# Two of four weight sums made by adding transfers, in a hybrid attention and convolution block on one core

## The chip, the core and the metric

One core of a Trainium2 chip runs one launch of the kernel. The metric is device time in microseconds (us) of that core. The kernel before the change took 2040.47 us, the median of 3 runs (2038.33 to 2040.82).

## What is computed

The block works on 256 rows of width 4096, all in float32. Cut to what matters here:

```
xn   = rms_norm(x, norm_in_g)
proj = xn @ w_in                                   # 4096 -> 14336 columns
q, k, v, z_a, a_c, g_c, z_c = split(proj)          # 2048 columns each
y_a = rms_norm(chunked_attention(q, k, v, rel_table)) * silu(z_a)
u   = causal_depthwise_conv31(a_c * sigmoid(g_c))
y_c = rms_norm(silu(layer_norm(u)) @ w_pw + b_pw) * silu(z_c)
h   = x + concat(y_a, y_c) @ w_out                 # 4096 x 4096
h   = h + sigmoid(rms_norm(h) @ w_ple_gate + b) * (p @ w_ple)
out = rms_norm(h) * final_g
```

Nearly all the work is matrix products of 256 rows with large weights that are read once each from HBM.

## The kernel before

**Precision.** Each float32 operand is split into a high part, rounded to the format that TensorE multiplies, and a low part, the rest. A product is three matmuls: high by high, low by high, high by low (`add`, line 365). For weights, `parts_of` (line 199) makes the parts: ScalarE (ACT) casts the tile to `wh` (line 204), VectorE (DVE) subtracts to get `wl` (line 205).

**Pairs.** `mixed_product` (line 327) computes two column blocks of 512 at once, for two halves of 128 rows. It walks over sixteen (for `w_pw` eight) *pairs*: two blocks of 128 rows of the weight matrix, `w0` and `w1`, each a tile of 128 x 2 x 512 with one row block and both column blocks. A pair is a 2 x 2 block product, taken in one of two ways:

- *plain*: eight block products, 24 matmuls (`add_plain`);
- *seven-product*, marked with a star in the orders: seven block products of sums (Winograd's form of Strassen's scheme), 21 matmuls. It needs sums of the activations (the `comb` tiles, made once) and four sums of weight blocks. With w0 = (a, b) and w1 = (c, d), columns side by side, these are a + b, b + d, a + b + d and a + b + d + c.

The sums were made on DVE: lines 426 and 427 write the first two into the tile `ua`, lines 430 and 431 the other two into `ub`. `pair_parts` (line 308) then splits each tile, `uh` by an ACT cast and `ul` by a DVE subtraction (again lines 204 and 205).

**Order.** Lists written out by hand say which pair comes when and which are seven-product; the eight-of-sixteen list used in most of the second half is

```
dense = units("1 0* 3 2* 5 4* 6* 7 8* 9 10* 11 12* 14* 13 15")
```

`first`, `early`, `early_six` and `late` put the marked pairs in the second half of a stage, mostly with a plain pair between two; `final` is like `dense` with seven marked pairs and three left to the end. In all, 122 of the pairs are seven-product ones. The stages are: the convolution's inputs (4 times), queries and keys (4), the pointwise product (2), the gates `z_a` and `z_c` (4, `dense`), `w_out` (4, the first in `late`) and `w_ple_gate` (4, the first in `late`, the last in `final`).

**Buffers.** Pools set how far loads and parts run ahead: `wpool` has 5 buffers for weight tiles `wt` and 3 each for `wh` and `wl`; `upool` has 2 buffers under each of the tags `u` (for `ua` and `ub`), `uh` and `ul`. Weight loads are asked for by SyncE (SP) in lines 403 and 190, in the order of its instruction stream; a load whose buffer is not free yet waits there, and so does all that stands behind it. A scheduler sets the order of each engine's instructions when the program is built, except where the source pins them. GpSimd (POOL) has little to do: a few powers for the norms (`rsqrt`, line 136), four memsets in the bias tiles (line 895).

Of the kernel before, what the change touches and what calls it, by code (L numbers as in the profile page):

```python
# [10 lines left out]
F32 = mybir.dt.float32  # L11
F32R = mybir.dt.float32r
AF = mybir.ActivationFunctionType
ALU = mybir.AluOpType
AX = mybir.AxisListType

P = 128
NB = 512
# [7 lines left out]
def hybrid_block(  # L26
# [23 lines left out]
    nc = tc.nc  # L50
# [17 lines left out]
    def pool(name, bufs, stack=ctx, side=0, **kw):  # L68
        return stack.enter_context(tc.tile_pool(name=name, bufs=bufs, side=sides[side], **kw))
# [13 lines left out]
    upool = pool("upool", 2, first_sums)  # L83
# [15 lines left out]
    def two_columns(w, kb, col, apart):  # L99

        rows = w[kb * P : (kb + 1) * P, :]
        return bass.AP(
            tensor=rows.tensor, offset=rows.offset + col,
            ap=[list(rows.ap[0]), [apart, 2], [1, NB]],
        )
# [76 lines left out]
    def fill(n):  # L182
        for _ in range(min(n, len(later))):
            later.popleft()()
# [123 lines left out]
    def pair_parts(src):  # L308

        tiles = [upool.tile([P, 2, NB], F32R, tag=tag, name=tag) for tag in ("uh", "ul")]  # L310
        return parts_of(src, 2, tiles)[0]

    def units(text):

        return [(int(u.rstrip("*")), u.endswith("*")) for u in text.split()]
# [3 lines left out]
    first = units("0 1 3 5 7 9 11 13 15 2* 8 4* 10 6* 12 14")  # L319
# [7 lines left out]
    def mixed_product(  # L327
        w, col, lhs, comb, order, on_helpers, ahead=None, fills=(0,), on_begin=None, apart=NB,
        left=(), begin=None,
    ):  # L330

        c = [[ps_acc.tile([P, NB], F32, tag="acc", name=f"acc{h}{j}") for j in range(2)] for h in range(NH)]
        helper = {}
        begun, ends = set(), {}  # L340
        n_left = len(left) // 2
        for n, (_, seven) in enumerate(order[: len(order) - n_left]):
            for name in ("P1", "P5", "P6", "P7", "P2", "P3", "P4") if seven else ("P2", "P3", "P4", "X"):
                ends[name] = n
        banks = {"P2": c[0][0], "P3": c[0][1], "P4": c[1][0], "X": c[1][1]}
        made, held = [], []

        def add_left(h, js, out=None, cols=slice(None)):


            for m in range(0, len(held), 2):
                for j in js:
                    dst = c[h][j] if out is None else out[:, cols]
                    for i, (kb, (wh, wl)) in enumerate(held[m : m + 2]):
                        xh, xl = block(kb, h)
                        for kind, (a, b) in enumerate(((xh, wh), (xl, wh), (xh, wl))):
                            pin(
                                nc.tensor.matmul(  # L358
                                    dst, a, b[:, j, cols],
                                    start=out is not None and m + i + kind == 0,  # L360
                                    stop=m + i + 1 == len(held) and kind == 2,
                                )
                            )

        def add(name, x, w2, n, final, kinds=range(3), then=lambda ins: None):

            for kind in kinds:
                a, b = ((x[0], w2[0]), (x[1], w2[0]), (x[0], w2[1]))[kind]
                made.append(
                    nc.tensor.matmul(  # L370
                        banks[name], a, b, start=name not in begun,
                        stop=final and ends[name] == n and kind == 2 and not (left and name in "P2 P3 P4"),
                    )
                )
                begun.add(name)
                then(made[-1])

        def block(kb, h):
            t = lhs[kb // 4]
            return [t[:, kb % 4, q, h * P : (h + 1) * P] for q in range(2)]  # L380

        def add_plain(n, k, wh, wl, **kw):
            pair = order[n][0]
            for j in range(2):
                for h in range(NH):
                    name = (("P2", "P3"), ("P4", "X"))[h][j]
                    add(name, block(2 * pair + k, h), (wh[:, j], wl[:, j]), n, k == 1, **kw)

        done, after = 0, ExitStack()
        if begin:  # L390
            done, behind = begin(add_plain)
            for ins in behind:
                after.enter_context(tc.issue_after(ins.ins))
        last_seven = max((n for n, (_, seven) in enumerate(order) if seven), default=None)
        for n, (pair, seven) in enumerate(order):
            if n < done:
                continue
            if ahead:
                ahead(pair)
            wts = []  # L400
            for k in range(2):
                wt = wpool.tile([P, 2, NB], F32, tag="w", name="wt")
                nc.sync.dma_start(wt, two_columns(w, 2 * pair + k, col, apart))
                wts.append(wt)
            if n >= len(order) - n_left:
                for k in range(2):
                    tiles = left[2 * (n - len(order) + n_left) + k]
                    held.append((2 * pair + k, parts_of(wts[k], 2, tiles and tiles())[0]))
                fill(fills[n % len(fills)])
                continue  # L410
            if not seven:
                for k in range(2):
                    add_plain(n, k, *parts_of(wts[k], 2)[0])
                fill(fills[n % len(fills)])
                continue
            begins = not helper
            if begins:
                for name in ("P1", "P5", "P7", "P6"):
                    helper[name] = ps_tmp.tile([P, NB], F32, tag="tmp", name=f"acc_{name}")
                banks.update(helper)  # L420
            w0, w1 = wts
            ua = upool.tile([P, 2, NB], F32, tag="u", name="ua")
            ub = upool.tile([P, 2, NB], F32, tag="u", name="ub")
            plus = partial(nc.vector.tensor_tensor, op=ALU.add)
            w0h, w0l = parts_of(w0, 1)[0]
            plus(ua[:, 0], w0[:, 0], w0[:, 1])  # L426
            plus(ua[:, 1], w0[:, 1], w1[:, 1])  # L427
            uah, ual = pair_parts(ua)
            w1h, w1l = parts_of(w1, 2)[0]
            plus(ub[:, 0], ua[:, 0], w1[:, 1])  # L430
            plus(ub[:, 1], ub[:, 0], w1[:, 0])  # L431
            ubh, ubl = pair_parts(ub)
            first = len(made)

            def s_of(i):
                t, at = comb[pair] if isinstance(comb, dict) else (comb[pair // 4], pair % 4)
                return [t[:, at + i // 2, q, (i % 2) * P : (i % 2 + 1) * P] for q in range(2)]

            k0, k1 = 2 * pair, 2 * pair + 1
            add("P1", block(k0, 0), (w0h[:, 0], w0l[:, 0]), n, True)  # L440
            add("P5", s_of(1), (uah[:, 0], ual[:, 0]), n, True)
            add("P7", s_of(0), (uah[:, 1], ual[:, 1]), n, True)
            add("P2", block(k1, 0), (w1h[:, 0], w1l[:, 0]), n, True)
            add("P3", s_of(3), (w1h[:, 1], w1l[:, 1]), n, True)
            add("P6", s_of(2), (ubh[:, 0], ubl[:, 0]), n, True)
            add("P4", block(k1, 1), (ubh[:, 1], ubl[:, 1]), n, True)
            if begins and on_begin:
                on_begin()
            if begins:
                tc.add_manual_dep(  # L450
                    made[first].ins, last_transpose[0].ins.name,
                    mybir.DependencyInfo(mybir.DependencyClass.NoSync, mybir.DependencyReason.DATA),
                    reason="transposes before the helpers take their banks",
                )
            if n == last_seven:
                on_helpers(helper)
            fill(fills[n % len(fills)])
        after.close()
        return (c, add_left) if left else c
# [73 lines left out]
    def first_pairs(add):  # L533
# [62 lines left out]
        for n in range(1, n_x + 1):  # L596
# [26 lines left out]
    rows = [(conv_ln_g, KCW), (conv_ln_b, KCW), (b_dw, KCW), (attn_out_g, AW // P),  # L623
            (conv_out_g, KCW), (ple_norm_g, KD)]
# [315 lines left out]
    for c0, order in zip(range(0, CW // NB, 2), point):  # L940
        row = broadcast_row(b_pw, c0 * NB, 2 * NB, tag="stage")
        rows = [row[:, j * NB : (j + 1) * NB] for j in range(2)]
# [191 lines left out]
    rows, fgs = [], []  # L1134

    def on_begin():
        rows.extend(broadcast_row(b_ple_gate, (c0 + j) * NB, NB) for j in range(2))
# [16 lines left out]
    for j in range(2):  # L1154
        wt = wpool.tile([P, 2, NB], F32, tag="w", name="wt")
# [115 lines left out]
```

## Time and profile before

| | us |
|---|---|
| median of 3 runs | 2040.47 |
| the profiled execution | 2039.1 |
| its span in the profile | 2037.3 |
| TensorE (PE) busy | 2019.6 (99%) |
| VectorE (DVE) busy | 1887.9 (93%) |
| ScalarE (ACT) busy | 1200.8 (59%) |
| GpSimd (POOL) busy | 8.1 |
| moved by the DMA engines | 412.29 MB, 202 GB/s over the span |

In a group's row of the profile stand the line, the engine, the operation, the tile written and those read, shapes and count; then busy us and the mean ns of one; then the idle time just before them on that engine and what ended it. A row of a wait table reads: who waited, for whom, us in total, times, longest. A row of the timeline: start, length, engine, line, operation, and in brackets an idle time before it. A row of DMA issues: tile and tensor, the issuing queue, count, KB of each, median us from issue to landing. PEld is TensorE's loading of weights, which runs beside its matmuls; a PE that is busy in the table can still be paced by something else, so the distance from one matmul's start to the next is read from the timeline.

### The profile page before, as it was taken

To read this page: it belongs to the slowest core of one execution; us is meant where nothing else is said; L and a number is where in the kernel's file an instruction comes from. 1 tells how busy PE (TensorE), PEld (TensorE's weight loads), DVE (VectorE), ACT (ScalarE), POOL (GpSimd) and SP (SyncE) were. 2 spreads that over 40 slices of the span, in tenths; PEclk is the share of its full clock that TensorE was granted. 3 is DMA by queue.
4 is the path that set the end of the run, shared out by engine and by line. 5 is a ranking of instruction groups with operands and counts; after the bars stand their busy time and mean duration, and the time that the engine had idled before them with its cause. 6 is when DMAs were issued, how large, how long until landed. Compare 5 with 4: busy or idle time off the path is not lost.

```text
span 2037.3 us, 26041 instructions
## 1 busy us (share of the span) xinstructions
PE 2019.6 (99%) x9106; PEld 1659.5 (81%) x9106; DVE 1887.9 (93%) x2688; ACT 1200.8 (59%) x1559; POOL 8.1 (0%) x19
## 2 busy tenths in 40 slices
PE   9999999999999999999999999999999999999997
PEld 7888888877888888888888888888888888888876
DVE  7999999799989998868899999999999999999998
ACT  7655546554565546676555656676565666655555
POOL 0000000000000000000000000000000000000000
PEclk9999999999999999999999999999999999999999
DMA  8666665666656665655666666676666656666765
GB/s 295 188 200 204 204 187 165 202 191 189 184 185 204 201 188 183 186 184 199 190 216 204 197 216 199 219 238 204 214 201 205 214 185 208 198 221 205 235 208 179
DMA packets 161853, 412.29 MB, mean 202 GB/s; under 512 B 12974, under 2 KB 16190, under 8 KB 161722
## 3 DMA queue, kind: packets, MB, share of 16 engines
q1 hardware_dynamic: 161072, 409.80, 63.3%
q8 instruction: 71, 1.16, 0.2%
q10 hardware_dynamic: 650, 0.84, 0.1%
q14 instruction: 60, 0.49, 0.1%
HBM read 406.39 MB, written 4.19 MB: 202 GB/s over the span
## 4 chain that ended last, share of the span: by engine, by line
PE 86%; DVE 10%; issue 2%; DMA 1%; ACT 1%; POOLq 0%; POOL 0%; ACTq 0%; DVEq 0%
PE acc L370 61%; PE acc_P L370 15%; PE acc L218 7%; DVE wl L205 4%; DVE cv L677 3%; DMA wt<-in_w_in_dram 1%; PE tmp_ps L170 1%; DVE ul L205 1%; PE tmp_ps L867 0%; PE tmp_ps L849 0%; ACT wh L204 0%; PE acc L358 0%; PE tmp_ps L834 0%; DVE z L492 0%; PE tmp_ps L872 0%
## 5 line engine op out<-in xcount | busy, mean ns | idle before, releaser
L370 PE MATMUL acc<-wh,big_t 128*128 128x512 f32 x3788 | 1172.1, 391 | 0.6 <-DVE z L988 0.3
L204 ACT CAST wh<-wt 128x1024 fp32r<-128x1024 f32 (+1 forms) x737 | 715.8, 982 | 543.0 <-PE acc L370 330.6
L205 DVE TENSOR_TENSOR wl<-wt,wh 128x1024 fp32r<-128x1024 f32 (+1 forms) x737 | 825.4, 1132 | 65.0 <-ACT wh L204 60.1
L370 PEld LDWEIGHTS acc<-wh,big_t 128*128 128x128 f32 x3788 | 708.4, 188 | 146.5 <-issue 0.6
L370 PE MATMUL acc<-wl,big_t 128*128 128x512 f32 x1894 | 731.1, 391 | 1.0 <-DVE wl L205 1.0
L370 PEld LDWEIGHTS acc<-wl,big_t 128*128 128x128 f32 x1894 | 355.2, 188 | 76.7 <-DVE wl L205 3.1
L677 DVE SCALAR_TENSOR_TENSOR cv<-uT,dw,cv 128x255 f32<-128x255 f32 (+23 forms) x480 | 204.9, 467 | 1.1
L204 ACT CAST uh<-ub 128x1024 fp32r<-128x1024 f32 x122 | 128.5, 1054 | 126.2 <-DVE ub L431 102.7
L218 PE MATMUL acc<-wh,big_t 128*128 128x512 f32 x560 | 173.1, 390 | 0.0
L204 ACT CAST uh<-ua 128x1024 fp32r<-128x1024 f32 x122 | 128.7, 1055 | 71.7 <-DVE ua L427 63.5
L205 DVE TENSOR_TENSOR ul<-ub,uh 128x1024 fp32r<-128x1024 f32 x122 | 149.0, 1221 | 8.8 <-ACT uh L204 7.8
L370 PE MATMUL acc_P<-uh,big_t 128*128 128x512 f32 x504 | 154.4, 392 | 0.0
L205 DVE TENSOR_TENSOR ul<-ua,uh 128x1024 fp32r<-128x1024 f32 x122 | 148.9, 1220 | 0.4 <-ACT uh L204 0.2
L218 PEld LDWEIGHTS acc<-wh,big_t 128*128 128x128 f32 x560 | 104.8, 188 | 21.4
L370 PEld LDWEIGHTS acc_P<-uh,big_t 128*128 128x128 f32 x504 | 93.3, 188 | 22.2 <-ACT uh L204 3.7
L218 PE MATMUL acc<-wl,big_t 128*128 128x512 f32 x280 | 109.1, 390 | 0.0
L426 DVE TENSOR_TENSOR ua<-wt 128x512 f32<-128x512 f32 x122 | 83.9, 688 | 25.9 <-DMA wt<-in_w_in_dram 19.0
L370 PE MATMUL acc_P<-ul,big_t 128*128 128x512 f32 x252 | 96.8, 392 | 0.0
L427 DVE TENSOR_TENSOR ua<-wt 128x512 f32<-128x512 f32 x122 | 83.7, 686 | 3.9 <-DMA wt<-in_w_in_dram 3.0
L431 DVE TENSOR_TENSOR ub<-ub,wt 128x512 f32<-128x512 f32 x122 | 83.8, 687 | 1.0
L430 DVE TENSOR_TENSOR ub<-ua,wt 128x512 f32<-128x512 f32 x122 | 83.7, 686 | 0.3
L370 PE MATMUL acc<-uh,big_t 128*128 128x512 f32 x244 | 75.4, 390 | 0.0
(241 smaller groups left out, 1523.0 us busy)
## 6 DMA issues: line engine op xcount, KB each, us to landing
wt<-in_w_in_dram SPq DMA_DIRECT2D x447, 512.0 KB, 4.0
wt<-in_w_out_dram SPq DMA_DIRECT2D x128, 512.0 KB, 4.2
wt<-in_w_ple_gate_dram SPq DMA_DIRECT2D x128, 512.0 KB, 4.2
wt<-in_w_pw_dram SPq DMA_DIRECT2D x32, 512.0 KB, 4.5
hc<-in_x_dram SPq DMA_DIRECT2D x8, 512.0 KB, 5.8
wt<-in_w_ple_dram SPq DMA_DIRECT2D x8, 512.0 KB, 4.2
xin<-in_x_dram SPq DMA_DIRECT2D x7, 512.0 KB, 8.2
out_dram<-hc SPq DMA_DIRECT2D x12, 256.0 KB, 2.4
```

Of the source, the lines that this page charges most:

```text
L170: nc.tensor.transpose(pt[:, i * T + h * P : i * T + (h + 1) * P], src[:, h, b * P : (b + 1) * P], ident,)
L204: nc.scalar.copy(wh[:, :kc, :], wt[:, :kc, :]),
L205: nc.vector.tensor_tensor(wl[:, :kc, :], wt[:, :kc, :], wh[:, :kc, :].bitcast(F32), ALU.subtract),
L218: nc.tensor.matmul(acc, a, b[:, k, :], start=kb == 0 and kind == 0, stop=kb == kblocks - 1 and kind == 2,)
L370: nc.tensor.matmul(banks[name], a, b, start=name not in begun, stop=final and ends[name] == n and kind == 2 and not (left and name in "P2 ...
L426: plus(ua[:, 0], w0[:, 0], w0[:, 1])
L427: plus(ua[:, 1], w0[:, 1], w1[:, 1])
L430: plus(ub[:, 0], ua[:, 0], w1[:, 1])
L431: plus(ub[:, 1], ub[:, 0], w1[:, 0])
L677: nc.vector.scalar_tensor_tensor(cv[:, i, PAD - k :], uT[:, i, : T + k - PAD], dw[:, b, k : k + 1], cv[:, i, PAD - k :], ALU.mult, ALU.add,)
```

## The change

Of the four sums of a seven-product pair, the first two (a + b and b + d) are no longer made on DVE. A plain transfer from SP loads (b, b) into `ua`, and a transfer from GpSimd that adds on writing puts (a, d) on top. The new function `sums_ahead(n)` asks for both for every seven-product pair among the next two in the order, right after the weight loads of pair n. As b of `w0` is not needed any more, only a of it is loaded. The other two sums are written over the first two in `ua`, after those have been split; `ub` is gone, and the two buffers of the tag `u` serve the `ua` of two pairs.

```diff
+        sums = {}
+
+        def sums_ahead(n):
+            for m in range(n, min(n + 3, len(order))):
+                if not order[m][1] or m in sums:
+                    continue
+                ua = sums[m] = upool.tile([P, 2, NB], F32, tag="u", name="ua")
+                rows = w[2 * order[m][0] * P : (2 * order[m][0] + 1) * P, :]
+                step = P * rows.ap[0][0]
+
+                def columns(first, step):
+                    return bass.AP(
+                        tensor=rows.tensor, offset=rows.offset + first,
+                        ap=[list(rows.ap[0]), [step, 2], [1, NB]],
+                    )
+
+                nc.sync.dma_start(ua, columns(col + apart, 0))
+                nc.gpsimd.dma_start(ua, columns(col, step + apart), accum_op=ALU.add)
...
-                nc.sync.dma_start(wt, two_columns(w, 2 * pair + k, col, apart))
+                if seven and k == 0:
+                    nc.sync.dma_start(wt[:, 0], w[2 * pair * P : (2 * pair + 1) * P, col : col + NB])
+                else:
+                    nc.sync.dma_start(wt, two_columns(w, 2 * pair + k, col, apart))
                 wts.append(wt)
+            sums_ahead(n)
...
-            ua = upool.tile([P, 2, NB], F32, tag="u", name="ua")
-            ub = upool.tile([P, 2, NB], F32, tag="u", name="ub")
+            ua = sums[n]
             plus = partial(nc.vector.tensor_tensor, op=ALU.add)
             w0h, w0l = parts_of(w0, 1)[0]
-            plus(ua[:, 0], w0[:, 0], w0[:, 1])
-            plus(ua[:, 1], w0[:, 1], w1[:, 1])
             uah, ual = pair_parts(ua)
             w1h, w1l = parts_of(w1, 2)[0]
-            plus(ub[:, 0], ua[:, 0], w1[:, 1])
-            plus(ub[:, 1], ub[:, 0], w1[:, 0])
-            ubh, ubl = pair_parts(ub)
+            plus(ua[:, 0], ua[:, 0], w1[:, 1])
+            plus(ua[:, 1], ua[:, 0], w1[:, 0])
+            ubh, ubl = pair_parts(ua)
```

## The prediction

> **What bounds the kernel now.** I read the page's engine shares first, then TensorE's own waits, then the chain of waits, to learn how much a lighter VectorE could return at all.
>
> ```profile
> span 2037.3 us, 26041 instructions
> PE 2019.6 (99%) x9106; PEld 1659.5 (81%) x9106; DVE 1887.9 (93%) x2688; ACT 1200.8 (59%) x1559; POOL 8.1 (0%) x19
> ```
> ```profile
> PEld acc_P L370 <- ACT uh L204: 4.7, 18, 0.5
> PEld acc_P L370 <- DVE ul L205: 4.0, 14, 0.6
> PEld acc L370 <- DVE wl L205: 3.1, 7, 1.2
> ```
> ```profile
> 1170.85 6.12 PE acc L370 x27
> ```
>
> The reader is to see that PE is the bound and nearly full: it is without work for 2037.3 - 2019.6 = 17.7 us, start and tail included. In the chain, 27 matmuls follow each other in 6.12 us, one per 0.227 us, and that pace hardly breaks. What VectorE (DVE) and ScalarE (ACT) owe PE in weight parts is 4.7 + 4.0 + 3.1 = 11.8 us of late weight loads, part of it hidden behind the matmul before. So a change that only unloads DVE can win a few us; I take 5, between 0 and 11.8. DVE is close behind, though, as three stretches show (columns: stretch; its length, then busy us of PE, PEld, DVE, ACT, POOL; granted clock, DMA share, GB/s):
>
> ```profile
> 0.00:60.00 60.00, 58.67 (x286) 46.88 (x287) 45.94 (x79) 44.65 (x87) 0.89 (x8) 1.00 0.81 272
> 1157.00:1239.00 82.00, 82.00 (x364) 67.91 (x363) 78.70 (x94) 49.59 (x55) 0.00 (x0) 1.00 0.65 206
> 1845.00:1930.00 85.00, 85.00 (x373) 69.26 (x372) 84.31 (x103) 49.13 (x59) 0.00 (x0) 1.00 0.68 214
> ```
>
> The second row is one stage in the order `dense`, eight seven-product and eight plain pairs. There the DMA engines are busy for 0.65 of the time. In the third, a gate stage, DVE works 84.31 of 85 us.
>
> **What the change removes.** Two of four sums in each of 122 pairs, lines 426 and 427:
>
> ```profile
> L426 DVE TENSOR_TENSOR ua<-wt 128x512 f32<-128x512 f32 x122 | 83.9, 688 | 25.9 <-DMA wt<-in_w_in_dram 19.0 <-DMA wt<-in_w_out_dram 4.9 <-DMA wt<-in_w_ple_gate_dram 1.1
> L427 DVE TENSOR_TENSOR ua<-wt 128x512 f32<-128x512 f32 x122 | 83.7, 686 | 3.9 <-DMA wt<-in_w_in_dram 3.0 <-DMA wt<-in_w_out_dram 0.7
> ```
>
> That is 83.9 + 83.7 = 167.6 us of DVE, 11 us per dense stage. It lies beside PE's work, so it returns only the 5 us above. The sums of lines 430 and 431 stay. Written over `ua`, they must now follow ACT's cast and DVE's subtraction that read `ua`; per pair the chain is cast 1.06, subtraction 1.22, two sums of 0.69, cast 1.06, subtraction 1.22 (the timeline rows below), some 5.7 us with their overlaps.
>
> **What it adds in bytes.** A pair loads 0.26 MB less for `w0`, 0.52 MB more for the plain half of `ua` and 0.52 MB more that is added: 0.79 MB, or 6.3 MB per dense stage. At 206/0.65 = 317 GB/s these take 19.8 us, and the DMA share goes from 0.65 to 0.89. Issuing from GpSimd takes no bytes off these engines. [...] No run here shows a GpSimd transfer yet.
>
> The first two `ua` loads stand in SP's queue between the loads of `x`. Four transfers, 2.1 MB, at 272/0.81 = 336 GB/s are 6 us; the first 60 us leave 0.19 x 60 = 11 us free. I cost that at nothing; without that cover it is at most 6 us.
>
> **What it adds in waits.** This is the term that decides. `upool` has two buffers for `ua`, so the `ua` of a pair can be asked for only when the last subtraction (`ul<-ub`) of the seven-product pair before the previous one is done. "Two pairs ahead" is the place in the source; in the order in which SP's instructions stand in the built program, a dense stage asks for the sums of 6* between the two loads of that same pair, and for 8*, 10* and 14* just ahead of their own pair's loads. From the release four things follow in a row: SP's issue, the plain load, GpSimd's issue, the adding transfer. The rows nearest to them:
>
> ```profile
> L403 SPq DMA_DIRECT2D wt<-in_w_in_dram x366: 327/367/371, 45.1 to 1306.2; - x183
> DMA to landing us min/median/max: 3.3/4.1/8.2
> ```
> ```profile
> wt<-in_w_in_dram SPq DMA_DIRECT2D x447, 512.0 KB, 4.0
> xin<-in_x_dram SPq DMA_DIRECT2D x7, 512.0 KB, 8.2
> ```
> ```profile
> L895 POOL MEMSET bias<- 64x256 f32 x4 | 1.2, 306 | 705.2 <-DMA bias<-in_rel_table_dram 477.9 <-ACT wh L204 227.3
> L139 POOL TENSOR_TENSOR r_x<-r_x,mhalf 128x2 f32<-128x2 f32 x1 | 1.0, 1009 | 58.9 <-DVE r_x L138 58.9
> ```
>
> An adding transfer and a GpSimd issue are in no row. Bounds: the adding transfer between the fastest plain one (3.3) and the slowest (8.2), GpSimd's issue between its cheapest instruction (0.3) and its dearest (1.0). Low end: 0.3 + 3.3 + 0.3 + 3.3 = 7.2 us; high end: 0.4 + 8.2 + 1.0 + 8.2 = 17.8. I take 0.4 + 4.0 + 1.0 + 8.2 = 13.6: for the adding one the `xin` row, since those loads ran at a DMA share of 0.81, nearest to the 0.89 worked out above.
>
> How much time the present schedule gives, in the dense stage above: for 6*, 10* and 14*, the release (end of `ul<-ub` of 2*, 6*, 10*), the cast that needs `ua`, the subtraction behind it, and PE's first use of that.
>
> ```profile
> 1176.75 1.22 DVE L205 TENSOR_TENSOR ul<-ub,uh 128x1024 fp32r<-128x1024 f32 x1
> ...
> 1190.81 1.22 DVE L205 TENSOR_TENSOR ul<-ua,uh 128x1024 fp32r<-128x1024 f32 x1
> ...
> 1193.68 1.22 DVE L205 TENSOR_TENSOR ul<-ub,uh 128x1024 fp32r<-128x1024 f32 x1
> ...
> 1205.50 1.22 DVE L205 TENSOR_TENSOR ul<-ua,uh 128x1024 fp32r<-128x1024 f32 x1
> ...
> 1210.58 1.22 DVE L205 TENSOR_TENSOR ul<-ub,uh 128x1024 fp32r<-128x1024 f32 x1
> ...
> 1225.47 1.23 DVE L205 TENSOR_TENSOR ul<-ua,uh 128x1024 fp32r<-128x1024 f32 x1
> ```
> ```profile
> 1189.07 1.06 ACT L204 CAST uh<-ua 128x1024 fp32r<-128x1024 f32 x1 [0.30 <-PE acc_P L370]
> ...
> 1204.03 1.06 ACT L204 CAST uh<-ua 128x1024 fp32r<-128x1024 f32 x1
> ...
> 1224.38 1.06 ACT L204 CAST uh<-ua 128x1024 fp32r<-128x1024 f32 x1 [0.26 <-PE acc_P L370]
> ```
> ```profile
> 1192.90 0.39 PE L370 MATMUL acc_P<-ul,big_t 128*128 128x512 f32 x1
> ...
> 1213.30 0.39 PE L370 MATMUL acc_P<-ul,big_t 128*128 128x512 f32 x1
> ...
> 1228.26 0.39 PE L370 MATMUL acc_P<-ul,big_t 128*128 128x512 f32 x1
> ```
>
> From release to cast: 1189.07 - 1177.97 = 11.1 us for 6*, 1204.03 - 1194.90 = 9.1 for 10*, 1224.38 - 1211.80 = 12.6 for 14*. From subtraction to PE: 0.9, 6.6 and 1.6 us, the slack. At 13.6 us: 6* is 13.6 - 11.1 = 2.5 late, PE waits 2.5 - 0.9 = 1.6. Its release stays 2.4 late (chain 5.7 against 5.8 now), 10* is 2.4 + 4.5 = 6.9 late, inside 6.6 plus the 1.6 that PE has lost already. The release of 10* makes up 2.1 (5.7 against 7.8), 14* is 4.8 + 1.0 = 5.8 late, and PE waits 5.8 - 1.6 - 1.6 = 2.6. Together 4.2 us per dense stage. Nine stages have that order and the last one nearly so: 42 us. The orders `early` and `late` space the marked pairs by a plain pair almost throughout, so I cost them at nothing.
>
> ```profile
> SPq L403 <- DVE wl L205: 1052.4, 478, 9.8
> ```
>
> Queued behind the waits: on ACT, behind the cast of `ua`, stand the `wh` casts of the next pairs, and on DVE their subtractions; that is why a late `ua` makes everything behind it late, and PE waits as soon as the slack is gone. On SP, a `ua` load that waits for its buffer holds back weight loads; the row above shows that SP stands waiting for DVE for half the span already, and the loads are in time. GpSimd's few other instructions (`r_x`, `r_c`, `r_h`, four memsets) stand among the adding transfers; behind `r_h` are sums from the third marked pair of the gate stage on, needed many pairs later: nothing.
>
> **Sum.** The profiled execution took 2039.1 us, span 2037.3 with 1.8 around it; the runs' median, 2040.47, is 1.4 above. 2039.1 + 42 - 5 = 2076 for that execution, and I forecast **2077** for a median.
>
> **Rivals.**
> - *Hidden, faster.* The place is the same chain; it decides at about 12 us from release to landing: PE is first touched by 6* at 11.1 + 0.9 = 12.0, by 14* at 12.2. For it: the low end is 7.2, and with plain times for both transfers (0.4 + 4.1 + 1.0 + 4.1 = 9.6) nothing outruns its slack. Then only the 5 us of late parts go: 2035.
> - *Hidden, no difference.* The same, but PE's own pace hides what DVE gives back: 2037 to 2044.
> - *DMA engines full.* If an added byte costs an engine twice a plain one, eight transfers of 0.52 MB add another 13 us per dense stage: share 0.89 + 0.16 = 1.05. No transfer is quick then, and at the high end, 17.8 us, the same walk gives 6* 5.8, 10* 2.9 and 14* 8.1 us of waiting: 17 us per stage, 170 in all, 2205. Against it: the rows show no engine time of an adding packet. [...]
> - *It does not run ahead.* Already in the forecast: SP's order undoes the two pairs of lead in dense stages.
>
> **How the numbers follow.** Slower with the chain at 12.3 to 16 us: 0.50. At 16 us the walk gives 11 us per stage, 2150. DMA engines full, above that: 0.20. Hidden and faster: 0.17. Hidden and within 0.2%: 0.13; 0.2% is 4 us, about what a measurement of this kernel can tell from no change. Range 2034 to 2180: it takes in about half of the faster case and half of the full-engine case, and leaves some 0.18 out. Faster 0.17, same 0.13, slower 0.70.
>
> **What would show it.** Right: ACT's `uh<-ua` casts waiting for the adding transfer in dense stages, PE waiting for `uh` and `ul` there, GpSimd transfers landing 8 us after issue, DMA share near 0.9. Wrong: landings near 4 us and no new PE wait (hidden), or a DMA share near 1.0 with all weight loads late (full engines). DVE should lose 167 us of busy time in every case.

## The result, and the profile after

The changed kernel takes **2198.67 us** (median of 6 runs, 2190.15 to 2223.04), the kernel before 2040.26 (6 runs, 2038.33 to 2040.82): a ratio of 1.0771, 95% interval 1.0749 to 1.0793, 158 us more. The forecast was 2077, its range 2034 to 2180. The direction was right, the size was not: the result lies 19 us above the range. The longest of the six runs had a lower granted clock (0.978) than the others (0.983 to 0.987) and is left out of the ratio. The profiled execution took 2198.76.

First the page of the changed kernel: engines, then the DMA queues (packets, MB, share of 16 engines' span).

```profile
span 2197.0 us, 26397 instructions
...
PE 2076.5 (95%) x9106; PEld 1665.9 (76%) x9106; DVE 1755.4 (80%) x2444; ACT 1188.9 (54%) x1559; POOL 168.0 (8%) x141
...
q1 hardware_dynamic: 190032, 441.79, 60.3%
q0 software_dynamic: 33184, 63.97, 18.2%
```

PE does the same 9106 matmuls, and now stands without work for 120.5 us where it stood for 17.7. VectorE is 132 us lighter and no longer close to the bound. The new queue q0 holds the adding transfers. It moves 63.97 MB in 0.182 x 16 x 2197.0 = 6398 us of engine time, 0.205 us per 2 KB; q1 needs 0.603 x 16 x 2197.0 = 21197 us for 441.79 MB, 0.098 us per 2 KB. **An added byte cost an engine 2.1 times a plain one.** That is the condition of the rival "DMA engines full", which took the factor as two; this trace shows the factor, and can't show the reason.

Next the issues (KB of each, median us from issue to landing). The weight tiles took 4.0 before.

```profile
wt<-in_w_in_dram SPq DMA_DIRECT2D x382, 512.0 KB, 4.7
...
ua<-in_w_in_dram SPq DMA_DIRECT2D x65, 512.0 KB, 4.9
ua<-in_w_in_dram POOLq DMA_DIRECT2D x65, 512.0 KB, 7.6
```

Then two dense stages in the table by stretches, in the columns of the prediction's. Before, such a stage was 82 us long with a DMA share of 0.65, 53 us of engine time. Now:

```profile
1133.00:1223.00 90.00, 84.75 (x360) 66.36 (x360) 69.38 (x76) 48.09 (x55) 9.74 (x8) 1.00 0.90 257
1223.00:1312.00 89.00, 84.33 (x361) 66.41 (x360) 69.44 (x77) 47.93 (x55) 9.74 (x8) 1.00 0.90 259
```

The share reads 0.90, close to the 0.89 forecast, but of a longer stage: 0.90 x 89 = 80 us of engine time. At the pace of before that would be 80 of 82 us. A share must be turned into time before two stages of different length are compared.

Who waits: ScalarE's cast of the first sums for the transfers, and PE for that cast.

```profile
ACT uh L204 <- DMA ua<-in_w_in_dram: 86.2, 31, 9.5
...
PE acc_P L370 <- ACT uh L204: 41.1, 29, 9.2
```

Matmul by matmul, the loss of 160 us between the two profiled executions stands here: 109 us in the ten stages in the orders `dense` and `final` (10.9 each), 11 in the two in `late` among them, 23 in the first pointwise stage, 14 in the first convolution stage, 3 net in all the rest. The stages in the orders `early` stay within 3 us each, nearly as forecast.

A look at 6* in the second of the two stages shows the chain (timeline; the release is the end of the first row):

```profile
1236.70 1.22 DVE L205 TENSOR_TENSOR ul<-ua,uh 128x1024 fp32r<-128x1024 f32 x1
...
1237.95 0.38 SPq L405 DMA_DIRECT2D ua<-in_w_in_dram  x1
...
1244.01 1.22 POOL L406 DMA_DIRECT2D ua<-in_w_in_dram  x1 [9.34 <-DVE wl L205]
...
1252.13 1.05 ACT L204 CAST uh<-ua 128x1024 fp32r<-128x1024 f32 x1 [2.95 <-DMA ua<-in_w_in_dram]
...
1256.93 1.05 ACT L204 CAST uh<-ua 128x1024 fp32r<-128x1024 f32 x1 [1.86 <-DVE ua L451]
1258.03 0.74 PE L370 MATMUL acc_P<-uh,big_t 128*128 128x512 f32 x2 [0.98 <-ACT uh L204]
```

From release to cast it is 1252.13 - 1237.92 = 14.2 us, forecast 13.6. PE stops briefly for the first sums at 1253.23, and again at 1258.03 for the larger ones, which are made only after the first have been split. That is the chain of the prediction, at about its length. But it does not stand at 6* and 14* alone. In the 86 seven-product pairs that follow the first one of the first `dense` stage, the cast starts within 0.2 us of the landing in 81%: four pairs in five wait for their own transfer. The table of line 406 says the same for the whole run (us waited, times), 77 of 122:

```profile
who waited for it (us, times):
  ACT uh L204: 229.6, 77
```

PE does not pay at each of them. Counted matmul by matmul, of the 109 us in the ten stages 32 stand at 6*, 24 at 14*, 23 at 8*, 21 at 10* and 9 at all other pairs. At 8* and 10* PE is mostly late at the plain parts of the pair's own tiles. Here is such a place at 10* (ScalarE, then PE):

```profile
1185.88 1.05 ACT L204 CAST uh<-ua 128x1024 fp32r<-128x1024 f32 x1 [2.76 <-DVE ua L451]
1186.83 2.94 ACT L204 CAST wh<-wt 128x1024 fp32r<-128x1024 f32 x3
```
```profile
1187.92 0.73 PE L370 MATMUL acc<-wh,big_t 128*128 128x512 f32 x2 [1.03 <-ACT wh L204]
```

The cast of the larger sums comes late, since line 451 makes them late, and the plain parts stand behind it on ScalarE.

### The profile page after: what moved, and what is told of

Same layout as the page of the kernel before. It is cut to its first block, busy times and chain, and to the rows that moved or that the text cites. A ratio compares the mean times of both kernels' runs of the same rounds, so it can differ in the third digit from the quotient of the medians.

```text
span 2197.0 us, 26397 instructions
## 1 busy us (share of the span) xinstructions
PE 2076.5 (95%) x9106; PEld 1665.9 (76%) x9106; DVE 1755.4 (80%) x2444; ACT 1188.9 (54%) x1559; POOL 168.0 (8%) x141
## 2 busy tenths in 40 slices
DMA packets 224000, 508.27 MB, mean 231 GB/s; under 512 B 16878, under 2 KB 20094, under 8 KB 223866
## 3 DMA queue, kind: packets, MB, share of 16 engines
q1 hardware_dynamic: 190032, 441.79, 60.3%
q0 software_dynamic: 33184, 63.97, 18.2%
## 4 chain that ended last, share of the span: by engine, by line
PE 49%; DMA 24%; DVE 14%; issue 7%; ACT 5%; ACTq 0%; SPq 0%; POOLq 0%; DVEq 0%; POOL 0%
PE acc L370 34%; PE acc L218 8%; DMA ua<-in_w_in_dram 8%; DMA ua<-in_w_out_dram 7%; DMA ua<-in_w_ple_gate_dram 6%; DVE wl L205 5%; PE acc_P L370 5%; DVE ul L205 3%; ACT uh L204 3%; DMA wt<-in_w_in_dram 2%; ACT wh L204 2%; DVE ua L451 1%; DVE ua L450 1%; DMA ua<-in_w_pw_dram 1%; DVE cv L697 1%
## 5 line engine op out<-in xcount | busy, mean ns | idle before, releaser
L370 PE MATMUL acc<-wl,big_t 128*128 128x512 f32 x1894 | 743.0, 395 | 15.2 <-DVE wl L205 15.0
L204 ACT CAST uh<-ua 128x1024 fp32r<-128x1024 f32 x244 | 256.3, 1051 | 487.9 <-DVE ua L451 222.4
L205 DVE TENSOR_TENSOR ul<-ua,uh 128x1024 fp32r<-128x1024 f32 x244 | 298.0, 1221 | 254.0 <-ACT uh L204 241.5
L697 DVE SCALAR_TENSOR_TENSOR cv<-uT,dw,cv 128x249 f32<-128x249 f32 (+23 forms) x480 | 201.2, 460 | 1.3
L406 POOL DMA_DIRECT2D ua<-in_w_in_dram x65 | 79.5, 1223 | 943.5 <-DMA ua<-in_w_in_dram 364.8
L218 PE MATMUL acc<-wl,big_t 128*128 128x512 f32 x280 | 109.0, 389 | 0.0
L450 DVE TENSOR_TENSOR ua<-ua,wt 128x512 f32<-128x512 f32 x122 | 83.6, 685 | 11.6 <-DMA wt<-in_w_in_dram 8.8
L451 DVE TENSOR_TENSOR ua<-ua,wt 128x512 f32<-128x512 f32 x122 | 83.9, 687 | 2.4
L370 PE MATMUL acc_P<-wh,big_t 128*128 128x512 f32 x244 | 75.7, 391 | 8.1 <-ACT wh L204 8.1
L370 PE MATMUL acc_P<-uh,comb_t 128*128 128x512 f32 x204 | 64.4, 397 | 6.9 <-ACT uh L204 6.9
L370 PEld LDWEIGHTS acc_P<-ul,big_t 128*128 128x128 f32 x252 | 48.5, 192 | 29.1 <-DVE ul L205 19.7
```

Source lines behind the costliest of these rows:

```text
L204: nc.scalar.copy(wh[:, :kc, :], wt[:, :kc, :]),
L205: nc.vector.tensor_tensor(wl[:, :kc, :], wt[:, :kc, :], wh[:, :kc, :].bitcast(F32), ALU.subtract),
L218: nc.tensor.matmul(acc, a, b[:, k, :], start=kb == 0 and kind == 0, stop=kb == kblocks - 1 and kind == 2,)
L370: nc.tensor.matmul(banks[name], a, b, start=name not in begun, stop=final and ends[name] == n and kind == 2 and not (left and name in "P2 ...
L406: nc.gpsimd.dma_start(ua, columns(col, step + apart), accum_op=ALU.add)
L450: plus(ua[:, 0], ua[:, 0], w1[:, 1])
```

## The experiments

Two theories. **Chain**: the sums are late because a buffer must come free and two transfers then run one behind the other; more lead cures it. **Load**: the DMA engines are full, so all landings are late. "w4" is `wpool` with 4 buffers in place of 5; it makes 4 KB of room per partition, where a run needs that. Each ratio is to the kernel before, run on the same chip. The code is cut to the lines that matter.

### 1 to 4: controls, a third buffer, and idle traffic

```diff
-    wpool = pool("wpool", 5)
+    wpool = pool("wpool", 4)              # e1 (on before), e2 (on after), e3, e4
-... upool.tile([P, 2, NB], F32, tag="u", name="ua")
+... upool.tile([P, 2, NB], F32, tag="u", name="ua", bufs=3)        # e3
+                t = upool.tile([P, 2, NB], F32, tag="spare", name="spare", bufs=1)
+                nc.gpsimd.dma_start(t, src)                        # e4, on before
+                nc.gpsimd.dma_start(t, src, accum_op=ALU.add)
```

> Control: the kernel before with 4 weight buffers in place of 5, which makes the room that the next runs need. Weight loads run one tile less ahead. Both theories: nearly nothing, 2040 to 2055 us.

> Control: the changed kernel with 4 weight buffers. Chain theory (the time is lost where a pair's sums can be asked for only when their buffer comes free, and then two transfers run one behind the other): the buffers of the sums are unchanged, so 2195 to 2220 us. Load theory (the added bytes, and the engine time of an adding transfer, make all loads late): one weight tile less ahead hurts more, 2220 to 2260.

> The changed kernel with a third buffer for the sums; the bytes are the same. Chain theory: the request comes one seven-product pair earlier, some 12 us in a dense stage, more than anything there was late; most of the 109 us that the ten dense stages lost comes back, and the 23 us of the first pointwise stage and 14 of the first convolution stage stay: 2080 to 2125 us. Load theory: the same bytes are moved, the loads stay late: 2180 to 2210.

> The kernel before, its sums on VectorE as before, and beside them a plain and an adding transfer of 512 KB for each seven-product pair into a tile that nobody reads, both from GpSimd, with the same place in the source as the real ones (1.05 MB more per pair; the change itself added 0.79). Nobody waits for them. Chain theory: within 0.7 per cent of the kernel before, 2040 to 2055 us. Load theory: most of the 158 us, 2140 us or more.

| run | us | ratio, interval |
|---|---|---|
| e1, before, w4 | 2049.8 | 1.0054, 1.0039 to 1.0069 |
| e2, after, w4 | 2213.58 | 1.0862, 1.0829 to 1.0896 |
| e3, after, w4, third buffer | 2112.3 | 1.0357, 1.0321 to 1.0393 |
| e4, before, w4, idle traffic | 2457.32 | 1.2061, 1.2021 to 1.2101 |

e2 falls into the range of the chain theory, not of the load theory. The third buffer brings back 101 of the 164 us between the controls, as the chain theory said. In the table of its line 406 ScalarE waits 19.9 us where it waited 222.8 in e2. Of the 44 us that e3 still loses in the ten dense stages, 38 stand ahead of PE's matmuls on the larger sums, some of them behind a weight tile that lands late, and next to nothing ahead of those on the first. The idle traffic says the opposite: nobody waits for it, and the kernel loses 408 us. Most of that is no load: in three stages GpSimd's `r_h`, `r_x` and a memset of the bias stand behind these transfers in its queue, and 239.1, 28.7 and 31.6 us are spent waiting for them. The largest in the groups of the page:

```profile
L1104 DVE SCALAR_TENSOR_TENSOR z<-acc_P,r_h,row 128x512 f32<-128x512 f32 x3 | 2.2, 747 | 239.1 <-POOL r_h L139 239.1
```

But the four z stages, where no such wait stands, lose 45 us, as much as in e2 (49). So neither theory holds alone.

### 5 to 8: release, addition, load, and two stages

```diff
-            plus(ua[:, 0], ua[:, 0], w1[:, 1])                     # e5
-            plus(ua[:, 1], ua[:, 0], w1[:, 0])
-            ubh, ubl = pair_parts(ua)
+            plus(w0[:, 1], ua[:, 0], w1[:, 1])
+            plus(w0[:, 0], w0[:, 1], w1[:, 0])
+            ubh, ubl = pair_parts(w0)
-                nc.gpsimd.dma_start(ua, columns(col, step + apart), accum_op=ALU.add)
+                nc.gpsimd.dma_start(ua, columns(col, step + apart))    # e6
+                nc.gpsimd.dma_start(onto, src, accum_op=ALU.add)   # e7, on before, w4
+        by_dma = begin is None and len(order) == 16                # e8
```

> The changed kernel, but the larger sums go into the w0 tile (its second half is empty, its first half has been split by then) and no longer over the first sums; no more room, the same bytes. Chain theory: the buffer comes free some 3 us earlier (two sums, a cast and a subtraction no longer hold it), about what 6* and 14* were late at the first sums; the dense stages keep the half that they lose at the larger sums: 2125 to 2165 us. Load theory: same bytes, 2190 to 2205.

> The changed kernel with the second transfer writing instead of adding; same bytes, queues and waits. It leaves out the additions of b, so the sums lack that part. A 2 KB packet of an adding transfer took 176 ns in the profile, a plain one 84. Chain theory: the second transfer lands some 2.5 us earlier, so much of the lateness at 6* and 14* goes, but not what the larger sums cost: 2125 to 2165 us. Load theory: engine time per dense stage falls by some 11 us of 92, loads are on time again: 2050 to 2110.

> The kernel before with 4 weight buffers, its sums on VectorE, and beside them one adding transfer of 640 KB from GpSimd per seven-product pair onto a tile that nobody reads: about the engine time that the change added net (a plain 256 KB and an adding 512 KB), without the backlog on GpSimd that the earlier spare transfers had. Chain theory: near its control of 2050, 2050 to 2065 us. Load theory: the dense stages lose 8 to 11 us each as in the earlier spare run, 2130 to 2165.

> The changed kernel with the sums by transfers only in the stages of sixteen pairs that have no begin step; the first convolution stage and the two pointwise stages make them on VectorE as before. Both theories of the dense stages are untouched by it. If the 14 and 23 us there come from sums that cannot be asked for early (the start, and a pool that opens only then), they come back whole: 2155 to 2170 us. If they are only wherever the load happens to surface, they turn up later: 2185 to 2205.

| run | us | ratio, interval | ten dense stages, us over before |
|---|---|---|---|
| after, unchanged | 2198.67 | 1.0771, 1.0749 to 1.0793 | 109 |
| e5 | 2200.78 | 1.0793, 1.0767 to 1.0818 | 124 |
| e6 | 2099.63 | 1.029, 1.0273 to 1.0307 | 40 |
| e7 | 2214.21 | 1.0877, 1.0838 to 1.0916 | 95 |
| e8 | 2172.51 | 1.0657, 1.0621 to 1.0692 | 105 |

e5 goes against the chain theory, but not cleanly: the weight tile is now held until the larger sums are split, and SP's weight loads wait for that in the z stages:

```profile
SPq L425 <- DVE ul L205: 106.1, 29, 10.1
```

e6 leaves every wait and byte in place and makes the second transfer a plain one; it leaves out the addition of b. It brings back 99 us, more than the chain theory allowed, and lands inside the range of the load theory. Its adding queue needs 9.7% of the engines where it needed 18.2%, and the transfers land in 5.8 us where they took 7.7 (medians of line 406).

e7 loses 95 us in the dense stages though no instruction of the work reads the transfers. But they ran back to back, ahead of the stages (GpSimd's line 403 waited 101 times, 819 us, for the transfer before), so by the author's estimate they load the engines harder than the change does, and another 45 us went in the first stage, where `r_x` waited behind them.

e8 shows the two other places. With the sums on VectorE the first convolution stage loses 0.4 us, not 14, the first pointwise stage 7, not 23. There the sums can't be asked for early: in the pointwise stage the pool of their buffers opens only then. But the stage behind the first convolution stage now loses 7 us where it lost nothing, so on balance only half of the 14 is gained; why, wasn't followed. The whole gains 26 us where 37 were expected.

### 9 to 12: the release alone, load in step, both cures, few transfers

```diff
+            ub = upool.tile([P, 2, NB], F32, tag="ub", name="ub", bufs=1)  # e9, w4
+            plus(ub[:, 0], ua[:, 0], w1[:, 1])
+            plus(ub[:, 1], ub[:, 0], w1[:, 0])
+            nc.gpsimd.tensor_copy(onto[:, 0, :1], ul[:, 0, :1].bitcast(F32))  # e10, on before, w4
+            nc.gpsimd.dma_start(onto, src, accum_op=ALU.add)
+        by_dma = [m for m, (_, seven) in enumerate(order) if seven][:2] if ... else []  # e12
```

> The changed kernel with 4 weight buffers and a tile of its own for the larger sums, so that the buffer of the first sums comes free some 3 us earlier and no weight tile is held longer; compare with the control of 2213.6. Chain theory: ScalarE waited 59 us for the first sums in the four z stages of the control, 2.7 us at a time; that goes, and with it more than half of the 116 us of the dense stages: 2130 to 2170 us. Load theory: same bytes, 2200 to 2220.

> The kernel before with 4 weight buffers and one adding transfer of 640 KB per seven-product pair that nobody reads, now asked for in step with the work: GpSimd copies one element of the pair's last weight part first, as the real transfers wait for such a release. The earlier spare transfers ran back to back, ahead of the stages, so they loaded the engines more than the change does. Chain theory: 2050 to 2065 us. Load theory: 2120 to 2165. Both at work, with the load's part as in the run with a third buffer (4 us of the 11 per dense stage): 2070 to 2100.

> The changed kernel with 4 weight buffers, the third buffer for the sums, and the sums on VectorE in the first convolution stage and the two pointwise stages. The two cures add up if their causes are separate: 2112 less 16 and 4 is 2092; 2085 to 2100 us. If one cause stands behind both: 2105 to 2120.

> Sums by transfers only for the first two marked pairs of a stage of sixteen pairs (not in the stages with a begin step, not in the pointwise ones), all others on VectorE. In the changed kernel these two had several us to spare in every dense stage. Chain theory: nothing waits for them, 2032 to 2045 us. Load theory: a quarter of the load, a quarter of the loss: 2060 to 2080.

| run | us | ratio, interval |
|---|---|---|
| e9 | 2202.27 | 1.0804, 1.0786 to 1.0822 |
| e10 | 2207.61 | 1.0812, 1.0772 to 1.0851 |
| e11 | 2109.32 | 1.0342, 1.0323 to 1.036 |
| e12 | 2168.91 | 1.0638, 1.0622 to 1.0653 |

**e9 fells the chain theory as it was stated.** The buffer comes free earlier, no weight tile is held, and the dense stages lose as much as in the control (123 us both). Ask to cast, in the pairs from the first `dense` stage on, goes from a median of 14.3 us in e2 to 17.3: the plain half now lands after 7.2 us (line 405, median) where it took 5.4, the adding one after 8.9 where it took 8.1. Asked earlier, the transfers take longer by as much, as a full resource would answer. The landing times, e2 and then e9, line 405 and then line 406:

```profile
DMA to landing us min/median/max: 3.6/5.4/9.8
...
DMA to landing us min/median/max: 5.9/8.1/11.4
```
```profile
DMA to landing us min/median/max: 3.8/7.2/9.8
...
DMA to landing us min/median/max: 5.9/8.9/10.9
```

e10 agrees: 158 us over its control, with nothing of the work reading those transfers. It has a flaw. The copy waits for the transfer before it and holds a weight part meanwhile; VectorE waited 31.6 us for that.

In e11 the two cures don't add up: 2109 against the 2092 expected of separate causes. The first pointwise stage loses 10 us and the first convolution stage 9 even so; what took the place there wasn't followed.

e12 misses for both theories, and shows the chain bare. Its DMA share in a dense stage is only 0.68, and still nine of the ten lose 5 to 9 us each, behind one long wait; these ten make half of its 129 us, and the other half wasn't followed. A dense stage in the table by stretches, and then what stands ahead of the stage that begins at 1223 (timeline; rows of SP, then GpSimd, then ScalarE):

```profile
1134.00:1223.00 89.00, 85.27 (x360) 69.10 (x359) 76.89 (x91) 49.20 (x56) 2.44 (x2) 0.96 0.68 209
```

```profile
1199.11 0.38 SPq L406 DMA_DIRECT2D ua<-in_w_in_dram  x1
...
1201.38 0.38 SPq L406 DMA_DIRECT2D ua<-in_w_in_dram  x1
```
```profile
1205.89 1.21 POOL L407 DMA_DIRECT2D ua<-in_w_in_dram  x1 [79.66 <-DVE z L494]
1213.24 1.22 POOL L407 DMA_DIRECT2D ua<-in_w_in_dram  x1 [6.14 <-issue]
```
```profile
1213.01 1.04 ACT L204 CAST uh<-ua 128x1024 fp32r<-128x1024 f32 x1 [9.62 <-DMA ua<-in_w_in_dram]
```

From asking to cast it is 13.9 us with engines a third idle: the length is the chain's own. VectorE's sums of the stage before hold both buffers until just before, so "two pairs ahead" is no lead at all. And the second adding transfer starts 7.35 us after the first, waiting for nothing that the profile shows ("issue"). In the changed kernel, e2, e3, e9, e11 and e12 none starts earlier than 0.26 us after the one before has landed; in e6, where they write, one starts up to 4.5 us before that. **The adding transfers went one at a time.** In the changed kernel that rarely decides: only 5 of its 122 start within 0.4 us of the landing before, where 37 do in e3.

### 13 to 16: which is it

```diff
 e13: e3 without accum_op
+            copied = nc.gpsimd.tensor_copy(tick[:, 0], ul[:, 0, :1].bitcast(F32))  # e14, e15
+            asked = nc.gpsimd.dma_start(onto, src, accum_op=ALU.add)   # e15: no accum_op
 e16:
-                nc.sync.dma_start(ua, columns(col + apart, 0))
-                nc.gpsimd.dma_start(ua, columns(col, step + apart), accum_op=ALU.add)
+                nc.gpsimd.dma_start(ua, columns(col, step + apart))
```

> The changed kernel with 4 weight buffers, a third buffer for the sums, and the second transfer writing instead of adding (the sums lack b). If the third buffer cures the chain and plain packets cure the engines, two causes, the dense stages come down to the control's: 2060 to 2080 us with the pointwise stage's loss left. If each cures the same thing, nothing is left to cure after the first: 2090 to 2110.

> The kernel before with 4 weight buffers and an adding transfer of 640 KB per seven-product pair onto a tile that nobody reads, in step with the pair (GpSimd first copies one element of the pair's last weight part into a tile of its own, which no longer waits for the transfer before). Engine theory: the dense stages lose 8 to 12 us each with nobody waiting, 2120 to 2170 us. Chain theory: 2050 to 2070.

> The same with transfers that write instead of adding: the same bytes and issues, about half the engine time. If the engines' time counts: most of the loss of the run with adding transfers goes, 2055 to 2085 us. If the bytes or GpSimd's issuing count: as with adding transfers, within 15 us of it. Chain theory: 2050 to 2065 for both.

> The changed kernel without the plain transfer of (b, b): one writing transfer of (a, d) from GpSimd per pair, so the sums lack b. The chain is one transfer, some 6 us, inside every slot of the walk, and the added bytes are 0.26 MB per pair. What VectorE's 168 us are worth by themselves: 2030 to 2045 us by the first step of the prediction. If even this is slower than 2050, the chain or GpSimd's issuing costs more than the walk had.

e13 and e16 leave out an addend, as e6 does. In the table, the last dense stage counts to the end of the run.

| run | us | ratio, interval | over its control | ten dense stages |
|---|---|---|---|---|
| e13 | 2078.06 | 1.0184, 1.0168 to 1.02 | 28 (e1) | 23 |
| e14 | 2196.42 | 1.0765, 1.0746 to 1.0785 | 147 (e1) | 116 |
| e15 | 2109.0 | 1.0333, 1.0312 to 1.0353 | 59 (e1) | 51 |
| e16 | 2051.04 | 1.0056, 1.0042 to 1.007 | 11 (before) | 5 |

e14 is the clean form of the load test, and it loses 147 us, more than the load theory's range. Its weight tiles are what is late now, so load alone can cost as much as the change, by another wait; ScalarE and VectorE wait for them (whole run):

```profile
ACT wh L204 <- DMA wt<-in_w_in_dram: 93.3, 66, 4.2
...
ACT wh L204 <- DMA wt<-in_w_ple_gate_dram: 68.4, 31, 5.1
```
```profile
DVE ua L444 <- DMA wt<-in_w_in_dram: 52.7, 28, 4.4
DVE ua L445 <- DMA wt<-in_w_in_dram: 26.0, 17, 4.4
```

One dense stage of e14, e15 and e3 in the table by stretches:

```profile
1230.00:1326.00 96.00, 87.06 (x363) 70.09 (x362) 77.81 (x93) 48.17 (x54) 17.59 (x17) 0.96 0.83 230
```
```profile
1104.00:1189.50 85.50, 82.63 (x361) 67.03 (x360) 78.07 (x93) 48.64 (x55) 15.64 (x17) 1.00 0.77 258
```
```profile
1110.00:1197.00 87.00, 83.36 (x362) 67.14 (x361) 69.97 (x77) 48.58 (x55) 9.74 (x8) 1.00 0.94 266
```

As engine time that is 96 x 0.83 = 80 us in e14, 85.5 x 0.77 = 66 in e15, 87 x 0.94 = 82 in e3, 80 in the changed kernel. e15 moves e14's bytes with e14's issues, at 14 us less of engine time per stage, and 87 of the 147 us come back. So it is engine time above all. But e15 lies above the 2055 to 2085 expected if engine time counts: the 59 us that stay belong to the bytes, to GpSimd's issuing or to its copy, and no run here separates these.

e3 answers the other half. It needs as much engine time as the changed kernel and loses less than half as much in the dense stages (45 us, the control 123). The engines are nearly full in both (shares 0.90 and 0.94); with a third buffer requests stand further ahead, the engines idle less, and the long landings (line 406, median 8.8 us, 7.7 in the changed kernel) are met. e13, with both cures, loses 28 us to its control where either alone leaves 60 or so: the cures overlap, but each does something that the other doesn't.

e16 is the ceiling of the idea as far as it was tried, and 2051 lies above the 2030 to 2045 expected. VectorE is as light as in the changed kernel, with half the added transfers and no addition, and the ten dense stages are still 5 us slower than before, not faster.

```profile
PE 2025.8 (99%) x9106; PEld 1663.3 (81%) x9106; DVE 1758.9 (86%) x2444; ACT 1198.8 (58%) x1559; POOL 101.3 (5%) x141
```

No run beat the kernel before, and none of these points to one that would.

## Why the prediction was wrong, step by step

1. *PE is the bound, and unloading VectorE can win 5 us at most.* The bound was right. The 5 us weren't there: e16 has the lighter VectorE almost free of cost and wins nothing.
2. *167.6 us less on VectorE.* The two sums went, but its busy time fell by 132.5. Durations of neighbours overlap in the records (a subtraction of 1.22 us is followed 1.14 us after its start), so their sum overstates what goes.
3. *Bytes, share 0.65 to 0.89.* This was worked out at plain rates: 20 us more engine time per dense stage. Measured 80 - 53 = 27. The bytes themselves were right, and issuing from GpSimd took none of them off the engines: 508.27 - 412.29 = 96 MB more on the pages' 16 engines, 122 pairs of 0.79, with q0's 63.97 MB among them. It was the rate that no row of before showed. The share of 0.90 that came out looks like a hit and is none, since the stage is longer.
4. *The start costs nothing, at most 6 us.* The `x` loads did become slower (8.2 to 11.9 us), and the first convolution stage lost 14. e8 gives that back in the stage itself, of which 7 us turn up in the next, and e3, e5 and e6 9 to 10 of it: that speaks for sums that are asked for late, at the end of that stage, and the loads of `x` weren't tested apart. The 23 us of the first pointwise stage were in no term, and the 11 in the two stages in `late` were put at nothing.
5. ***This is the step that failed: "Together 4.2 us per dense stage."*** The chain itself was sized nearly right, 13.6 us against a median of 14.6. But the walk took its durations as fixed and its slots from the schedule of before, and it priced only PE's stop for the first sums, so it found two waits: 1.6 us at 6* and 2.6 at 14*. Measured are 3.2 at 6*, 2.3 at 8*, 2.1 at 10*, 2.4 at 14* and 0.9 elsewhere: 10.9 per stage, 109 in ten, for 42. The walk was right at 14*, half at 6*, and had nothing for 8* and 10*. A lateness isn't made up behind 6* but carried from pair to pair: the engines, with 80 us of work in an 82 us stage, answer an earlier request with a later landing (e9: the plain half after 7.2 us, e2 5.4). The walk was also steep: with 14.6 in place of 13.6 it gives 2.6 + 4.6 = 7.2 us per stage, so one us of error in the chain was worth 30 us in ten stages.
6. *GpSimd's queue and SP's order cost nothing.* SP's order undid the lead, as said. In GpSimd's queue adding transfers stand one behind the other; in 5 of 122 cases that holds one back here, and no run prices it.
7. *Larger sums, chain of 5.7 us.* It was only used for the release. PE also stops a second time for it (1258.03 above), and at the plain parts that stand behind it on ScalarE (1187.92 above); neither was priced. In the trace some 44 of the 109 us stand behind late casts of larger sums and some 34 behind late casts of first sums. So this second half of the failed step is the larger one, though the larger sums are late in part because the first were.

Together: 2199 - 2077 = 122 us were missed. The dense stages make 109 - 42 = 67 of them, the stages put at nothing or in no term 14 + 23 + 11 + 3 = 51, and the 5 us of gain that didn't come the rest. The signs that the prediction named for itself came all but one (casts and PE waiting, landings of 7.6 us, a share of 0.90; VectorE fell by 132 us, not 167), but they would have come at 42 us as at 109.

Of the rivals, "DMA engines full" at 2205 had the mechanism (an added byte at twice a plain one's engine time, 2.1 times as measured) and came within 7 us of the result. It got 0.20, because no row of before showed an adding packet: there its factor of two was an assumption. Its own walk, 17 us per dense stage and nothing elsewhere, is not what happened (10.9 per stage, 50 us elsewhere). Its share above 1 wasn't reached either: 27 us of added engine time, not 33. That its number came so close is in part luck.

## What to carry to other kernels

Before moving work to the DMA engines, add up their time per stage (share x length) beside the time of the stage; a kernel at 0.65 has less room than it seems when an added byte costs 2.1 times a plain one, as here. When the sum comes near the stage's length, as with 80 of 82 us here, latencies measured before the change need not hold (weight tiles landed after 4.7 us in place of 4.0), and a walk with fixed durations finds a few late pairs where most will be late. Such a walk has to price every first use behind a late tile, also of tiles that only stand behind it in an engine's queue. A request "n pairs ahead" in the source is only as early as its buffer and its place in the issuing queue.

## What the hardware showed that was not expected

- **PE's granted clock fell with its pauses.** It did with each of the seven pauses of over 2 us (the longest 9.2), and with some shorter ones: a window inside such a stretch, 959.0 to 968.8 us, reads 0.50; wider windows read 0.66 behind the first pause of the pointwise stage, and 0.72 in a gate stage.

```profile
962.00:972.00 10.00, 5.63 (x16) 4.17 (x16) 4.43 (x5) 3.00 (x3) 1.23 (x1) 0.66 0.71 190
...
1911.00:1923.00 12.00, 6.92 (x20) 4.67 (x19) 6.00 (x6) 3.99 (x4) 1.21 (x1) 0.72 0.74 195
```

  Matmuls then started 0.427 us apart, not 0.227, in stretches of 3.4, 6.8 or 10.2 us: 12 of them in the changed kernel, none before, beside one at the tail in both. In the 12 stretches 106 matmuls started; at 0.2 us more each, some 21 us of the 158 are slow matmuls, not waiting. (The mean clock, which fell from 0.998 to 0.984, would give (0.016 x 2197.0) - (0.002 x 2037.3) = 31 us, but it counts the pauses inside these stretches too.)
- **Adding transfers from GpSimd went one at a time**, the next 0.26 us or more after the landing of the last (changed kernel, e2, e3, e9, e11, e12); writing ones overlapped, by up to 4.5 us (e6). What makes them wait, the profile doesn't show. GpSimd's issue took 1.21 us for an adding transfer and 0.72 for a writing one (medians of line 406, after and e6).
